# Down projection as seven products, with left factors made beside gate/up and kept in DRAM

## The chip, the cores and the metric

One core of a Trainium2 chip runs the whole program. The metric is the time of one execution in microseconds (us) of device time.

## The reference

The reference is one layer of a streaming encoder, for 1024 prompt rows and 8 x 16 sample rows (1152 rows in all, D = 1024). The change is in its last part, the feed-forward block with 2816 features and the norm behind it:

```python
out = h + (jax.nn.silu(hf @ w_gate) * (hf @ w_up)) @ w_down
y_prompt = rmsnorm(xp, g_final)
y_sample = rmsnorm(xs, g_final)
```

Here `hf` is the normed `h`. Everything is fp32.

## The kernel before

**Products.** Each fp32 operand is split into a high part (ScalarE copies it to the type fp32r, L129) and a low part (VectorE subtracts the high part, L130). `mma` (L881 to L883) then issues three matmuls for each product: high by high, high by low, low by high. The 1152 rows are nine token tiles of 128, or three chunks of 384.

**Gate and up, 1050 to 1518 us.** `swiglu(f0)` handles two of the 22 feature tiles, in 11 steps of 264 matmuls of 384 columns. On chunks 0 and 1 it multiplies by the seven-product form: `head` and `tail` make seven products of quarter matrices in place of eight, with sums and differences of weight quarters (A11, A12, A22, S1 to S4) on one side and of activation quarters (B11, B21, B22, T1 to T4) on the other. Chunk 2 is multiplied plainly (`plain`). `gate` and `up` make the activation `fsg`, and GpSimd's queue stores its six pieces of 128 x 384 per step in the DRAM tensor `a_d` (L1077).

**Down, 1520 to 1799 us.** The products run over two groups of token tiles (5, then 4) and, for each, two halves `dh` of 512 output columns. A pass takes the 22 feature tiles in pairs. For each pair it loads and splits 128 x 1024 of `w_down` (`wd`). In a group's first pass it also loads and splits the activations of that pair from `a_d` (`ar`, into `a`), which stay in SBUF for the second pass. Each token tile has its own PSUM bank (`ps_d`), and takes 22 x 3 matmuls of 512 columns per pass: 9 x 2 x 22 x 3 = 1188 in all. `done(t)` then adds the bank to `y` (L1127), squares and sums on ScalarE (L1131), makes the scale (L1133, L122, a power on GpSimd), scales `y` (L1135) and stores it. In the last pass the last six feature tiles are done token tile by token tile, so that the four tiles finish one after another.

**Order.** A scheduler places each engine's instructions by priority before the run, and each engine then executes its own list in that order. Weight loads and splits get priority over what stands up to `PRI_W` places before them, as far as their buffers allow. A load into a buffer waits until its last reader is done. The pools `wraw`, `whi` and `wlo` (three buffers each) hold weights in all phases; `dp`, `ap2`, `yq` hold `a`, `ar` and `y`. Loads and the stores of `y` are issued on the SyncE queue, in order.

## Time and profile before

| | |
|---|---|
| median of 3 runs | 1797.46 us (1795.79 to 1801.07) |
| profiled execution | 1801.29 us |
| its span, first to last instruction | 1799.5 us |
| mean granted TensorE clock | 0.995 |
| busy share of TensorE, VectorE, ScalarE | 98%, 55%, 33% |

The span is the time that the trace covers; the 1.8 us beside it lie outside any instruction. All times of the trace below are of that one execution. A share of busy time is a mean over the whole program, and single stretches differ from it.

### The profile page before, as it was taken

The page shows a single profiled execution, that of the slowest core. Times are in us where ns is not written, and L with a number is a line of the kernel's source. Part 1 is how long each engine was busy: PE and PEld are TensorE (multiplying, and loading weights), DVE is VectorE, ACT ScalarE, POOL GpSimd, SP SyncE. Part 2 cuts the span into 40 slices and gives each one's busy share as a digit, 9 for nine tenths or more (in the row PEclk, how much of TensorE's full clock was granted, in tenths as well). Part 3 has the DMA queues.
Part 4 walks back from the last instruction along what each step waited for, and adds up shares of the span by engine and source line. Part 5 has one row for each costly group of instructions (what it writes and reads, how often), then busy time and mean ns, then how long its engine had stood idle before and what let it go on. Part 6 is the DMA issues. An engine that isn't in the chain of part 4 may idle for free.

```text
span 1799.5 us, 26106 instructions
## 1 busy us (share of the span) xinstructions
PE 1766.8 (98%) x10503; PEld 1667.8 (93%) x10503; DVE 995.6 (55%) x1739; ACT 600.3 (33%) x1074; POOL 157.0 (9%) x266
## 2 busy tenths in 40 slices
PE   7999999999999999899999899999999999999998
PEld 6998888999999999899999899999999999888886
DVE  6337778464999672543527666555555554433423
ACT  5235556332434322410315423222222222322321
POOL 1020000111121111000001100000000000000000
PEclk9999999999999999999999999999999999999999
DMA  7412112474666435672224311222222224734522
GB/s 220 84 50 70 62 64 67 161 193 140 200 190 194 141 110 144 192 251 86 84 70 152 104 65 62 74 74 74 74 74 74 74 74 158 243 102 158 202 97 70
DMA packets 197285, 214.80 MB, mean 119 GB/s; under 512 B 19699, under 2 KB 162263, under 8 KB 197020
## 3 DMA queue, kind: packets, MB, share of 16 engines
q1 hardware_dynamic: 181228, 161.97, 29.8%
q0 software_dynamic: 15936, 51.17, 8.1%
q8 instruction: 82, 1.34, 0.3%
q14 instruction: 39, 0.32, 0.1%
HBM read 156.63 MB, written 57.39 MB: 119 GB/s over the span
## 4 chain that ended last, share of the span: by engine, by line
PE 92%; DMA 3%; DVE 2%; issue 1%; ACT 1%; POOL 0%; SPq 0%; POOLq 0%; ACTq 0%; DVEq 0%
PE ps_mm L153 11%; PE ps_mm L155 11%; PE ps_mm L154 11%; PE ps_c L882 5%; PE ps_c L883 5%; PE ps_c L881 5%; PE ps_d L881 5%; PE ps_d L882 5%; PE ps_d L883 5%; PE ps_b L883 3%; PE ps_b L882 3%; PE ps_b L881 3%; PE ps_h L883 2%; PE ps_h L881 2%; PE ps_h L882 2%; PE ps_a L881 2%
## 5 line engine op out<-in xcount | busy, mean ns | idle before, releaser
L881 PE MATMUL ps_d<-wd_h,a 128*128 128x512 f32 x396 | 154.7, 391 | 2.1 <-ACT a L129 2.1
L882 PE MATMUL ps_d<-wd_l,a 128*128 128x512 f32 x396 | 154.9, 391 | 0.0
L883 PE MATMUL ps_d<-wd_h,a 128*128 128x512 f32 x396 | 153.5, 390 | 0.0
L130 DVE TENSOR_TENSOR wd_l<-wd_r,wd_h 128x1024 fp32r<-128x1024 f32 x44 | 54.0, 1226 | 152.2 <-ACT wd_h L129 152.2
L129 ACT ACTIVATE wd_h<-wd_r 128x1024 fp32r<-128x1024 f32 x44 | 46.6, 1060 | 181.8 <-PE ps_d L883 160.5
L153 PE MATMUL ps_mm<-T_x,wx_h 128*128 128x384 f32 x288 | 100.0, 347 | 0.0
L155 PE MATMUL ps_mm<-T_x,wx_l 128*128 128x384 f32 x288 | 97.3, 338 | 0.0
L154 PE MATMUL ps_mm<-T_x,wx_h 128*128 128x384 f32 x288 | 97.0, 337 | 0.0
L881 PEld LDWEIGHTS ps_d<-wd_h,a 128*128 128x128 f32 x396 | 74.8, 189 | 18.1 <-ACT a L129 2.5
L882 PEld LDWEIGHTS ps_d<-wd_l,a 128*128 128x128 f32 x396 | 74.8, 189 | 15.7
L883 PEld LDWEIGHTS ps_d<-wd_h,a 128*128 128x128 f32 x396 | 74.6, 188 | 15.4
L1077 POOL DMA_DIRECT2D a_d<-fsg x66 | 35.7, 541 | 478.4 <-DVE fsg L1076 473.1
L1049 DVE TENSOR_TENSOR u<-ps_c,u 128x384 f32<-128x384 f32 x44 | 24.4, 555 | 81.5 <-PE ps_c L883 81.3
L153 PE MATMUL ps_mm<-T_x,wga_h 128*128 128x384 f32 x192 | 65.9, 343 | 0.0
L155 PE MATMUL ps_mm<-T_x,wz_l 128*128 128x384 f32 x192 | 65.2, 340 | 0.0
L153 PE MATMUL ps_mm<-T_x,wz_h 128*128 128x384 f32 x192 | 64.9, 338 | 0.0
L155 PE MATMUL ps_mm<-T_x,wga_l 128*128 128x384 f32 x192 | 64.9, 338 | 0.0
L154 PE MATMUL ps_mm<-T_x,wz_h 128*128 128x384 f32 x192 | 64.8, 338 | 0.0
L153 PE MATMUL ps_mm<-T_x,wgs_h 128*128 128x384 f32 x192 | 64.8, 338 | 0.0
L154 PE MATMUL ps_mm<-T_x,wga_h 128*128 128x384 f32 x192 | 64.7, 337 | 0.0
L154 PE MATMUL ps_mm<-T_x,wgs_h 128*128 128x384 f32 x192 | 64.7, 337 | 0.0
L155 PE MATMUL ps_mm<-T_x,wgs_l 128*128 128x384 f32 x192 | 64.5, 336 | 0.0
(1050 smaller groups left out, 5246.2 us busy)
## 6 DMA issues: line engine op xcount, KB each, us to landing
wd_r<-in_w_down_dram SPq DMA_DIRECT2D x44, 512.0 KB, 3.7
a_d<-fsg POOLq DMA_DIRECT2D x66, 192.0 KB, 2.2
wfg_r<-in_w_gate_dram SPq DMA_DIRECT2D x22, 512.0 KB, 4.1
wfu_r<-in_w_up_dram SPq DMA_DIRECT2D x22, 512.0 KB
acB<-ac_d SPq DMA_DIRECT2D x9, 1024.0 KB, 7.8
ar<-a_d SPq DMA_DIRECT2D x11, 640.0 KB, 5.3
xbc_d<-cv POOLq DMA_DIRECT2D x36, 192.0 KB, 2.1
xb<-xbc_d SPq DMA_DIRECT2D x9, 768.0 KB, 6.4
```

The lines of the kernel that those rows point to most:

```text
L129: act.activation(hi, src, AF.Copy)
L130: vec.tensor_tensor(out=lo, in0=src, in1=hi.bitcast(F32), op=ALU.subtract)
L153: pe.matmul(out, ah, bh, start=(i == 0), stop=False)
L154: pe.matmul(out, ah, bl, start=False, stop=False)
L155: pe.matmul(out, al, bh, start=False, stop=(i == n - 1))
L881: pe.matmul(ps, ah, bh, start=start and i == 0, stop=False, skip_group_check=True)
L882: pe.matmul(ps, ah, bl, start=False, stop=False, skip_group_check=True)
L883: pe.matmul(ps, al, bh, start=False, stop=stop and i == n - 1, skip_group_check=True)
L1049: add = lambda out, ps, x: vec.tensor_tensor(out=out, in0=ps, in1=x, op=ALU.add)
L1077: st(out=a_d[(f0 + i) * P:(f0 + i + 1) * P, c * CW:(c + 1) * CW], in_=t)
```

## The change

The down projection becomes seven products over blocks of a 2 x 2 form: feature halves (11 tiles each), pairs of token tiles (`tA` = 0, 1, 2, 6 and `tB` = 3, 4, 5, 7), and column halves `D1`, `D2`. The order is A11, A12, S1, S4, S2, S3, A22. Each product has 11 steps, and a step has four tile pairs of three matmuls of 512 columns. Tile 8 is multiplied plainly, as a fifth part of the steps of A11, A12, S1 and S4. A11 and A12 share four banks, S1 and S4 another four; S2, S3 and A22 go on adding into a third set of four (printed as `ps_S2`), which is read out after each of the three.

The left factors (sums and differences of activation blocks) are made by `factors` in the gate/up steps, which now pair feature tile f0 with f0 + 11, and are stored in the DRAM tensor `fa_d`, tile 8 in `a8_d`: 16 stores per step in place of 6. Each weight load of gate/up becomes two loads of 256 KB. The buffers of the earlier phases' weights and PSUM are freed ahead of the down phase. In the down phase a step loads 128 x 512 of the left factor and of `w_down` into one `raw` buffer (five of them), and splits both (four `hi` and `lo` buffers). The right factors T1 to T4 are made from `w_down` in place (`t1` to `t4`, by `sub`), with T1 and T2 held in `kept`. Before their last block, products run step by step; the last two steps run tile by tile.

```diff
+HF = NF // 2
+FACTORS = ("A11", "A12", "A22", "S1", "S2", "S3", "S4")
...
-    a_d = dram.tile([FF, T], F32, name="a_d")
+    fa_d = dram.tile([7, HF * P, 512], F32, name="fa_d")
+    a8_d = dram.tile([FF, P], F32, name="a8_d")
...
-            fp = ph2.enter_context(tc.tile_pool(name="fp", bufs=13, reuse_waits="tile"))
+            fp = ph2.enter_context(tc.tile_pool(name="fp", bufs=11, reuse_waits="tile"))
...
-                        ld(out=view(r), in_=src[kh * 512:(kh + 1) * 512, f0 * P:(f0 + 2) * P]
-                           .rearrange("(k p) c -> p k c", p=P))
+                        for j in range(2):
+                            f = (j * HF + f0) * P
+                            ld(out=view(r)[:, :, j * P:(j + 1) * P],
+                               in_=src[kh * 512:(kh + 1) * 512, f:f + P].rearrange("(k p) c -> p k c", p=P))
...
-                    st(out=a_d[(f0 + i) * P:(f0 + i + 1) * P, c * CW:(c + 1) * CW], in_=t)
+                    if i == 1 and c == 2:
+                        factors(*(sg[j, 2][:, n * P:(n + 1) * P] for n in range(2) for j in range(2)), 3 * P, "fs")
+                        for j in range(2):
+                            f = (j * HF + f0) * P
+                            st(out=a8_d[f:f + P, :], in_=sg[j, 2][:, 2 * P:])
+                    elif i == 1 and c == 0:
+                        factors(*(sg[j, n] for n in range(2) for j in range(2)), 0, "ft")
+                def factors(a11, a12, a21, a22, c0, tag):
+                    w = a11.shape[1]
+                    s2_, s3, s4 = (fp.tile([P, w], F32, tag=tag, name=n, bufs=11 if tag == "ft" else 4)
+                                   for n in ("fs2", "fs3", "fs4"))
+                    vec.tensor_tensor(out=s3, in0=a11, in1=a21, op=ALU.subtract)
+                    s1_ = a21
+                    vec.tensor_tensor(out=s1_, in0=a21, in1=a22, op=ALU.add)
+                    vec.tensor_tensor(out=s2_, in0=s1_, in1=a11, op=ALU.subtract)
+                    vec.tensor_tensor(out=s4, in0=a12, in1=s2_, op=ALU.subtract)
+                    for n, x in enumerate((a11, a12, a22, s1_, s2_, s3, s4)):
+                        st(out=fa_d[n, f0 * P:(f0 + 1) * P, c0:c0 + w], in_=x)
...
-            for f0 in range(0, NF, 2):
+            for f0 in range(HF):
...
-        psum_pools(ph, t=5)
...
-        for t0, n in ((0, 5), (5, 4)):
...
+        psum_pools(ph, t=8)
+        def pool(name, bufs=1, **kw):
+            return ph.enter_context(tc.tile_pool(name=name, bufs=bufs, reuse_waits="tile", **kw))
+        fraw, yq, fhl = pool("fraw", 5, side="right"), pool("yq", NT, side="right"), pool("fhl", 4, side="right")
+        xp, keep, yp = pool("xp", 3), pool("keep"), pool("yp", 2)
+        kept = keep.tile([P, HF, 512], F32, name="kept")
+        p1 = [keep.tile([P, 512], F32, name=f"dp1_{p}") for p in range(4)]
+        tA, tB = (0, 1, 2, 6), (3, 4, 5, 7)
+        D1, D2 = slice(0, 512), slice(512, 1024)
+        sub = lambda out, a, b: vec.tensor_tensor(out=out, in0=a, in1=b, op=ALU.subtract)
+        gfB = yp.tile([P, D], F32, name="gfB", bufs=1)
+        ys, sss = [], {}
+        def wd(i, j, f):
+            return w_down[0, (i * HF + f) * P:(i * HF + f + 1) * P, j * 512:(j + 1) * 512]
+        def xload(src, name):
+            x = xp.tile([P, 512], F32, tag=name[:2], name=name)
+            ld(out=x, in_=src)
+            return x
+        def product(left, right, ps, start, stop, a8=None, e=None, estart=False, estop=False, begin=None):
+            steps = []
+            r0 = 512 if a8 is None else 512 + P
...
+            def mm(f, n):
+                h, l, (xh, xl) = steps[f]
+                if n < 4:
+                    c = slice(n * P, (n + 1) * P)
+                    mma(bank_of(n), [(h[:, c], l[:, c], h[:, r0:r0 + 512], l[:, r0:r0 + 512])],
+                        start and f == 0, stop and f == HF - 1)
+                elif a8 is not None:
+                    c = slice(512, r0)
+                    mma(e, [(h[:, c], l[:, c], xh, xl)], estart and f == 0, estop and f == HF - 1)
+            for f in range(HF):
+                with tc.high_priority(max(0, min(PRI_W, tc.cur_priority - pri0[0]))):
+                    raw = fraw.tile([P, 1152], F32, tag="raw", name=f"{left}_{f}_r")
+                    hi = fhl.tile([P, 1152], F32R, tag="hi", name=f"{left}_{f}_h")
+                    lo = fhl.tile([P, 1152], F32R, tag="lo", name=f"{left}_{f}_l")
+                    ld(out=raw[:, :512], in_=fa_d[FACTORS.index(left), f * P:(f + 1) * P, :])
+                    if a8 is not None:
+                        ld(out=raw[:, 512:r0], in_=a8_d[(a8 * HF + f) * P:(a8 * HF + f + 1) * P, :])
+                    rs = slice(r0, r0 + 512)
+                    at, other = right(f, raw[:, rs]) or (None, None)
+                    if at is None:
+                        split(hi[:, :r0 + 512], lo[:, :r0 + 512], raw[:, :r0 + 512])
                     else:
...
+                        split(hi[:, :r0], lo[:, :r0], raw[:, :r0])
+                        split(hi[:, rs], lo[:, rs], at)
+                    x = hi[:, rs], lo[:, rs]
+                    if other is not None:
+                        x = tuple(xp.tile([P, 512], F32R, tag=f"x{n}", name=f"x{n}_{f}") for n in "hl")
+                        split(*x, other)
+                steps.append((hi, lo, x))
+                if f < HF - 2:
+                    for n in range(5):
+                        mm(f, n)
+                if begin is not None and f == 5:
+                    begin()
+            for n in range(5):
+                mm(HF - 2, n)
+                mm(HF - 1, n)
+                yield n
+        def add(t, cols, x):
+            vec.tensor_tensor(out=ys[t][:, cols], in0=x, in1=ys[t][:, cols], op=ALU.add)
+        def square(t, cols):
+            if t not in sss:
+                sss[t] = sm.tile([P, 2], F32, tag="ssf", name="ssf", bufs=NT)
+            n = cols.start // 512
+            sq = yp.tile([P, 512], F32, tag="sq", name="sqf")
+            act.activation(sq, ys[t][:, cols], AF.Square, accum_out=sss[t][:, n:n + 1])
+        def finish(t):
+            ss, y = sss[t], ys[t]
+            vec.tensor_tensor(out=ss[:, 0:1], in0=ss[:, 0:1], in1=ss[:, 1:2], op=ALU.add)
+            r = rstd_of(ss[:, 0:1], 1)
+            vec.scalar_tensor_tensor(out=y, in0=y, scalar=r, in1=gfB, op0=ALU.mult, op1=ALU.mult)
+            ld(out=y_prompt[0, t * P:(t + 1) * P, :] if t < NT - 1 else ys_flat, in_=y)
...
+        def plain(i, j):
+            def right(f, r):
+                ld(out=r, in_=wd(i, j, f))
+            return right
+        def t1(f, r):
+            b11, b12 = xload(wd(0, 0, f), "ba"), xload(wd(0, 1, f), "bb")
+            sub(kept[:, f, :], b12, b11)
+            return kept[:, f, :], b12
+        def t2(f, r):
+            ld(out=r, in_=wd(1, 1, f))
+            sub(kept[:, f, :], r, kept[:, f, :])
+            return kept[:, f, :], None
+        def t3(f, r):
+            ld(out=r, in_=wd(1, 1, f))
+            sub(r, r, xload(wd(0, 1, f), "bb"))
+        def t4(f, r):
+            ld(out=r, in_=wd(1, 0, f))
+            sub(r, r, kept[:, f, :])
+        def total(p, ps):
+            u = yp.tile([P, 512], F32, tag="u", name="du")
+            vec.tensor_tensor(out=u, in0=ps, in1=p1[p], op=ALU.add)
+            return u
+        a, c, b = ([None] * 4 for _ in range(3))
+        e = bank("t", "ps_e1")
+        for n in product("A11", plain(0, 0), a, True, False, a8=0, e=e, estart=True, begin=load_y):
+            if n < 4:
+                act.activation(p1[n], a[n], AF.Copy)
+        for n in product("A12", plain(1, 0), a, False, True, a8=1, e=e, estop=True):
+            if n < 4:
+                add(tA[n], D1, a[n])
+                square(tA[n], D1)
+            else:
+                add(8, D1, e)
+                square(8, D1)
+        e = bank("t", "ps_e2")
+        for n in product("S1", t1, c, True, False, a8=0, e=e, estart=True):
+            if n < 4:
+                add(tB[n], D2, c[n])
+        for n in product("S4", plain(1, 1), c, False, True, a8=1, e=e, estop=True):
+            if n < 4:
+                add(tA[n], D2, c[n])
+            else:
+                add(8, D2, e)
+                square(8, D2)
+                finish(8)
+        for n in product("S2", t2, b, True, False):
+            if n < 4:
+                add(tA[n], D2, total(n, b[n]))
+                square(tA[n], D2)
+                finish(tA[n])
+                add(tB[n], D1, p1[n])
+        for n in product("S3", t3, b, False, False):
+            if n < 4:
+                add(tB[n], D2, total(n, b[n]))
+                square(tB[n], D2)
+        for n in product("A22", t4, b, False, True):
+            if n < 4:
+                add(tB[n], D1, b[n])
+                square(tB[n], D1)
+                finish(tB[n])
```

Three places of VectorE's list follow. The first is where the third product into a set of banks follows the second (S3 to A22). `A22_k_r`, `_h` and `_l` are the raw, high and low buffers of step k; `du` is the sum that `total` makes from a bank; numbers at the end count the tiles. Before, at the end of a pass, the list had this:

```order
L130 TENSOR_TENSOR wd5_1_0_l_15399<-wd5_1_0_r_15396,wd5_1_0_h_15398 128x1024
L130 TENSOR_TENSOR wd5_1_2_l_15429<-wd5_1_2_r_15426,wd5_1_2_h_15428 128x1024
L1127 TENSOR_TENSOR y5_15130<-ps_d_14990,y5_15130 128x512
L1127 TENSOR_TENSOR y6_15132<-ps_d_14991,y6_15132 128x512
L1127 TENSOR_TENSOR y7_15134<-ps_d_14992,y7_15134 128x512
L1127 TENSOR_TENSOR y8_15136<-ps_d_14993,y8_15136 128x512
L130 TENSOR_TENSOR wd5_1_4_l_15459<-wd5_1_4_r_15456,wd5_1_4_h_15458 128x1024
L130 TENSOR_TENSOR wd5_1_6_l_15489<-wd5_1_6_r_15486,wd5_1_6_h_15488 128x1024
L130 TENSOR_TENSOR wd5_1_8_l_15519<-wd5_1_8_r_15516,wd5_1_8_h_15518 128x1024
```

Now it has this, where products A22 and S3 meet:

```order
L1135 TENSOR_TENSOR A22_5_r_16222<-A22_5_r_16222,kept_14359 128x512
L1246 TENSOR_TENSOR du_16080<-ps_S2_15568,dp1_0_14360 128x512
L1246 TENSOR_TENSOR du_16092<-ps_S2_15572,dp1_1_14361 128x512
L134 TENSOR_TENSOR A22_2_l_16164<-A22_2_r_16162,A22_2_h_16163 128x1024
L1198 TENSOR_TENSOR y3_14514<-du_16080,y3_14514 128x512
L1135 TENSOR_TENSOR A22_6_r_16242<-A22_6_r_16242,kept_14359 128x512
L1198 TENSOR_TENSOR y4_14516<-du_16092,y4_14516 128x512
L134 TENSOR_TENSOR A22_3_l_16184<-A22_3_r_16182,A22_3_h_16183 128x1024
L1246 TENSOR_TENSOR du_16104<-ps_S2_15576,dp1_2_14362 128x512
L1246 TENSOR_TENSOR du_16116<-ps_S2_15580,dp1_3_14363 128x512
```

The reads of the four banks (L1246) are no longer a group by themselves: two splits, a `sub` and two additions stand between the second and the third of them.

The second place is where S3 follows S2, again on VectorE; `bb` is the second block of `w_down` that T3 needs. The counterpart before is the list shown first.

```order
L134 TENSOR_TENSOR S3_1_l_15880<-S3_1_r_15878,S3_1_h_15879 128x1024
L1246 TENSOR_TENSOR du_15786<-ps_S2_15568,dp1_0_14360 128x512
L1135 TENSOR_TENSOR S3_5_r_15966<-S3_5_r_15966,bb_15971 128x512
L1246 TENSOR_TENSOR du_15805<-ps_S2_15572,dp1_1_14361 128x512
L1198 TENSOR_TENSOR y0_14508<-du_15786,y0_14508 128x512
L1198 TENSOR_TENSOR y1_14510<-du_15805,y1_14510 128x512
L1246 TENSOR_TENSOR du_15824<-ps_S2_15576,dp1_2_14362 128x512
L1135 TENSOR_TENSOR S3_6_r_15988<-S3_6_r_15988,bb_15993 128x512
L1246 TENSOR_TENSOR du_15843<-ps_S2_15580,dp1_3_14363 128x512
L134 TENSOR_TENSOR S3_2_l_15902<-S3_2_r_15900,S3_2_h_15901 128x1024
```

Here the `sub` of S3_6, which needs the raw buffer that S3_1's split gives back, stands ahead of the read of the fourth bank.

The third place is the end of VectorE's list. Before:

```order
L1133 TENSOR_TENSOR ssf_15381<-ssf_15381 128x1
L1135 SCALAR_TENSOR_TENSOR y5_15130<-y5_15130,rs_r_15678,gfB_14216 128x1024
L122 TENSOR_SCALAR rs_v_15704<-ssf_15381 128x1
L1127 TENSOR_TENSOR y7_15134<-ps_d_15394,y7_15134 128x512
L1135 SCALAR_TENSOR_TENSOR y6_15132<-y6_15132,rs_r_15706,gfB_14216 128x1024
L1133 TENSOR_TENSOR ssf_15385<-ssf_15385 128x1
L122 TENSOR_SCALAR rs_v_15732<-ssf_15385 128x1
L1135 SCALAR_TENSOR_TENSOR y7_15134<-y7_15134,rs_r_15734,gfB_14216 128x1024
L1127 TENSOR_TENSOR y8_15136<-ps_d_15395,y8_15136 128x512
L1133 TENSOR_TENSOR ssf_15389<-ssf_15389 128x1
L122 TENSOR_SCALAR rs_v_15760<-ssf_15389 128x1
L1135 SCALAR_TENSOR_TENSOR y8_15136<-y8_15136,rs_r_15762,gfB_14216 128x1024
```

Now, with L1198 adding, L1209 and L126 making the scale's input and L1211 scaling:

```order
L1198 TENSOR_TENSOR y5_14518<-ps_S2_15576,y5_14518 128x512
L1209 TENSOR_TENSOR ssf_16095<-ssf_16095 128x1
L1211 SCALAR_TENSOR_TENSOR y3_14514<-y3_14514,rs_r_16330,gfB_14364 128x1024
L126 TENSOR_SCALAR rs_v_16344<-ssf_16095 128x1
L1198 TENSOR_TENSOR y7_14522<-ps_S2_15580,y7_14522 128x512
L1209 TENSOR_TENSOR ssf_16107<-ssf_16107 128x1
L1211 SCALAR_TENSOR_TENSOR y4_14516<-y4_14516,rs_r_16346,gfB_14364 128x1024
L126 TENSOR_SCALAR rs_v_16360<-ssf_16107 128x1
L1209 TENSOR_TENSOR ssf_16119<-ssf_16119 128x1
L126 TENSOR_SCALAR rs_v_16376<-ssf_16119 128x1
L1211 SCALAR_TENSOR_TENSOR y5_14518<-y5_14518,rs_r_16362,gfB_14364 128x1024
L1211 SCALAR_TENSOR_TENSOR y7_14522<-y7_14522,rs_r_16378,gfB_14364 128x1024
```

The scalings of three tiles (y4, y5, y7) now stand behind the last addition from a bank; before, only that of the last tile (y8) did.

## Rows read from the trace of the kernel before

**Rows 1.** The page: span, and busy time by engine.
```profile
span 1799.5 us, 26106 instructions
PE 1766.8 (98%) x10503; PEld 1667.8 (93%) x10503; DVE 995.6 (55%) x1739; ACT 600.3 (33%) x1074; POOL 157.0 (9%) x266
```

**Rows 2.** The page: chain that ended last, by engine.
```profile
PE 92%; DMA 3%; DVE 2%; issue 1%; ACT 1%; POOL 0%; SPq 0%; POOLq 0%; ACTq 0%; DVEq 0%
```

**Rows 3.** Windows: busy us and instructions by engine, granted clock, DMA share, GB/s.
```profile
core 0: us, PE busy (x) PEld busy (x) DVE busy (x) ACT busy (x) POOL busy (x), PEclk, DMA share, GB/s
1050.00:1300.00 250.00, 250.00 (x1432) 250.00 (x1431) 145.53 (x219) 68.10 (x90) 17.82 (x33) 1.00 0.23 75
...
1518.40:1520.60 2.20, 0.07 (x2) 0.04 (x1) 1.86 (x4) 2.20 (x3) 0.54 (x1) 1.00 0.15 49
1520.60:1526.00 5.40, 5.40 (x17) 4.29 (x18) 2.84 (x3) 1.08 (x1) 0.00 (x0) 0.68 0.96 313
...
1592.60:1661.00 68.40, 68.40 (x303) 56.66 (x302) 25.00 (x25) 22.46 (x29) 0.00 (x0) 1.00 0.41 139
...
1728.00:1791.40 63.40, 63.40 (x282) 52.45 (x280) 20.48 (x26) 14.29 (x23) 1.65 (x3) 1.00 0.22 73
```

**Rows 4.** Waits of 1520 to 1800 us: total, times, longest.
```profile
ACT wd_h L129 <- PE ps_d L883: 160.5, 37, 5.7
...
ACT a L129 <- DMA ar<-a_d: 11.4, 6, 5.7
```

**Rows 5.** PE's order of time around the start of the down phase.
```profile
1518.10 0.34 PE L883 MATMUL ps_c<-T_h,wfu_l 128*128 128x384 f32 x1
1520.57 0.50 PE L881 MATMUL ps_d<-wd_h,a 128*128 128x512 f32 x1 [2.13 <-ACT a L129]
```

**Rows 6.** Groups of 1520 to 1800 us, shapes apart: busy, mean ns, idle before.
```profile
L130 DVE TENSOR_TENSOR wd_l<-wd_r,wd_h 128x1024 fp32r<-128x1024 f32 x42 | 51.5, 1226 | 149.3 <-ACT wd_h L129 149.3
L129 ACT ACTIVATE wd_h<-wd_r 128x1024 fp32r<-128x1024 f32 x41 | 43.5, 1060 | 161.2 <-PE ps_d L883 160.5 <-DMA y<-h_d 0.7
L130 DVE TENSOR_TENSOR a<-ar,a 128x1280 fp32r<-128x1280 f32 x11 | 16.2, 1491 | 10.7 <-ACT a L129 10.5
...
L1127 DVE TENSOR_TENSOR y<-ps_d,y 128x512 f32<-128x512 f32 x18 | 12.2, 687 | 9.4 <-PE ps_d L883 9.3
L1135 DVE SCALAR_TENSOR_TENSOR y<-y,rs_r,gfB 128x1024 f32<-128x1024 f32 x9 | 11.5, 1281 | 1.5 <-POOL rs_r L124 1.5
...
L1133 DVE TENSOR_TENSOR ssf<-ssf 128x1 f32<-128x1 f32 x9 | 1.4, 152 | 1.4 <-ACT sqf L1131 1.4
```

**Rows 7.** Groups of earlier stretches: smaller tensor operations, the stores, a weight's split.
```profile
L763 DVE TENSOR_TENSOR t<-t,yb 128x512 f32<-128x512 f32 x16 | 10.3, 681 | 0.0
...
L130 DVE TENSOR_TENSOR ohl<-oc,ohl 128x128 fp32r<-128x128 f32 x12 | 2.7, 288 | 10.2 <-ACT ohl L129 10.2
...
L1077 POOL DMA_DIRECT2D a_d<-fsg x66 | 35.7, 541 | 478.4 <-DVE fsg L1076 473.1
...
L129 ACT ACTIVATE wfu_h<-wfu_r 128x1024 fp32r<-128x1024 f32 x20 | 21.2, 1061 | 20.0 <-PE ps_c L882 20.0
```

**Rows 8.** DMA issues: count, KB each, median us from issue to landing.
```profile
wd_r<-in_w_down_dram SPq DMA_DIRECT2D x44, 512.0 KB, 3.7
...
y<-h_d SPq DMA_DIRECT2D x9, 512.0 KB, 6.6
...
oc<-o_d SPq DMA_DIRECT2D x3, 256.0 KB, 4.3
...
h<-in_x_sample_dram SPq DMA_DIRECT2D x1, 512.0 KB, 10.2
```

**Rows 9.** A window of 2 us in which the DMA engines were full.
```profile
1530.00:1532.00 2.00, 2.00 (x10) 1.67 (x9) 1.37 (x2) 0.85 (x2) 0.00 (x0) 1.00 1.05 421
```

**Rows 10.** PE's last matmul and VectorE's last rows, in order of time.
```profile
1788.32 1.28 DVE L1135 SCALAR_TENSOR_TENSOR y<-y,rs_r,gfB 128x1024 f32<-128x1024 f32 x1
1789.51 0.15 DVE L1133 TENSOR_TENSOR ssf<-ssf 128x1 f32<-128x1 f32 x1
...
1791.37 0.39 PE L883 MATMUL ps_d<-wd_h,a 128*128 128x512 f32 x1
...
1794.40 1.28 DVE L1135 SCALAR_TENSOR_TENSOR y<-y,rs_r,gfB 128x1024 f32<-128x1024 f32 x1 [0.73 <-POOL rs_r L124]
```

83 lines of the change are left out of this document (16 added, 67 removed).

## The prediction

> **What bounds the kernel now.** I read the page first: TensorE is busy 1766.8 of 1799.5 us [rows 1], and the chain of work that ended last lies on it for 92% [rows 2]. The windows say the same for both stretches that the change touches: in gate/up 250.00 of 250.00 us, and in the middle of the down phase 68.40 of 68.40 us, at a granted clock of 1.00, the upper of the two levels [rows 3]. VectorE and ScalarE have room there: 25.00 and 22.46 us of 68.40. The waits show the direction: ScalarE waits 160.5 us for matmuls to give weight buffers back, and only 11.4 us for the loads of activations [rows 4]. So in the down phase TensorE sets the pace and the others follow. From 1592.6 to 1661 us a matmul takes 68.40 / 303 = 0.226 us.
>
> The profiled execution took 1801.29 us, 1.8 more than its span, and the median of the runs is 3.8 lower. I sum against the span of 1799.5 and take off 2.0 for the median.
>
> **What it removes.** 1188 matmuls become 7 x 4 x 11 x 3 = 924, and 4 x 11 x 3 = 132 for tile 8: 1056. The 132 fewer are worth 132 x 0.226 = **29.8 us**, as long as nobody keeps TensorE waiting. A step of four tiles is now 12 x 0.226 = 2.71 us, one with tile 8 is 3.39. The rest asks whether the others keep that pace.
>
> **Gate/up: 0.** Per step (264 matmuls; 250 us hold 1432, so 46 us) VectorE gets four operations on 384 columns, at no more than the 0.68 of 512 columns, and four on 128 columns at about 0.29 [rows 7]: at most 3.9 us on 145.53 / 250 x 46 = 26.8 us [rows 3]. GpSimd gets 16 stores of 0.54 us [rows 7], 8.7 us of 46. No instruction of gate/up reads a factor back, and the down phase begins with the oldest ones. Weight loads become 256 KB in 512-byte rows; a 256-KB load landed in 4.3 us [rows 8], and today the split of those weights waits for TensorE and never for its load [rows 7]. So this work lies beside the matmuls. If that cover failed at some steps, 3 us in all; the term is 0 to +3, and I take 0.
>
> **The start: -1.** Today TensorE idles 2.1 us for ScalarE's first `a` [rows 5], and its clock then falls: 0.68 in the next 5.4 us [rows 3], worth 5.4 x 0.32 = 1.7. Now the raw and high parts of the first steps can be ready before gate/up ends, since their buffers lie over activations that are done earlier. VectorE has, after the last gate/up matmul, one product of 384 columns (at most 0.68), three of 128 columns (0.29 each) and the low part of A11_0, 1152 columns wide: between 1.23 and 1.49, so 1.36 [rows 6]. That is 2.9 us, and five high-by-high matmuls (1.1 us) run in it. The idle becomes about 1.6 us, in two pieces. With the clock lost as today it is -0.5, without -2.2, with one late load +3. I take -1.
>
> **Inside the seven products: +7.** Now each product loads and splits both factors anew. VectorE per step: A11, A12, S4 one split of 1152 columns, 1.36 us of 3.39; S1 three splits and a `sub`, 2.9 of 3.39; S2 two splits and a `sub`, 2.0 of 2.71; S3 and A22 one split of 1024 (1.23) and a `sub` (0.68), 1.9 of 2.71 [rows 6, 7]. To S3 and A22 come four scalings (1.28), 16 reads and additions (0.69) and eight small operations (0.15): 22 x 1.91 + 5.1 + 11.0 + 1.2 = 59.3 us in 22 x 2.71 = 59.6. VectorE's rows follow each other some 0.08 us closer than their lengths (1788.32 + 1.28 against 1789.51, rows 10), which gives about 6 us back. So VectorE has next to no room there, and where it comes late in its list's order TensorE waits.
>
> Where S3 ends, the list shows a wait that no speed of the loads removes. A22_2 needs the buffers of S3_9 (four of them, in turn), which are free when S3's last block ends. Then follow ScalarE's high part (1.06) and A22_2_l (1.23), an addition, a `sub`, an addition, A22_3_l, and only then the third `du`. From the end of S3: 1.06 - 0.6 for the earlier end of S3_9, then 1.15 + 0.61 + 0.60 + 0.61 + 1.15 + 0.69 = 5.3 us. TensorE wants that bank (A22_0, third tile) 6 x 0.226 = 1.36 us after S3's end. It waits **3.9 us**.
>
> Where S2 ends, the `sub` of S3_6 stands ahead of the fourth `du`. Its load can start when S3_1_l is done, at about 1.3 us before S2's end; with 4.3 us of landing [rows 8] the `sub` ends 3.7 us after that end and the `du` 0.6 later, where TensorE wants it at 2.0: 2.3 us late. With 2 us of landing there is no wait; with 6.6, the time of a `y` load in traffic [rows 8], it is 4.6. Further on S3_5 stands behind three scalings and two `sub`s, 0 to 3 us late; I take 1. The sum is 3.9 + 2.3 + 1, about 7, with 3 (the list alone, fast loads) and 16 (6.6 us at the five links of this kind) as ends.
>
> The DMA engines carry it. The down phase moves 77 + 99 loads of 256 KB, 44 of 64 KB, `y`, `gfB` and the output, about 59 MB, in 248 us: 238 GB/s, where full engines gave 421 [rows 9]. S3 is densest: 33 loads, 8.7 MB, and 2 MB of output in 30 us, 360 GB/s.
>
> **The tail: +1.6.** Today the last matmul starts at 1791.37 and the last scaling ends at 1795.68 [rows 10], 3.9 us after that matmul's end; the store takes the remaining 3.8. Now three scalings stand behind the last addition: by the list, 0.85 us after the end VectorE is free of y3, and then an addition 0.61, 1.2, small ones 0.5, 1.2 and 1.28, 5.5 us in all. Bounds are 1 and 4, the latter with four stores at once.
>
> **Sum:** 1799.5 - 29.8 + 0 - 1 + 7 + 1.6 = 1777.3; less 2.0 gives **1775** us. With all favourable ends it is 1797.5 - 29.8 - 2.2 + 3 + 1 = 1769.5, and the pace of a matmul (0.225 to 0.227) moves that by 0.1 only; with the unfavourable ones 1797.5 - 29.8 + 3 + 3 + 16 + 4 = 1793.7.
>
> **Rivals.**
> *The chain of late steps is longer (0.2).* In S3, and in S1 where VectorE has 0.5 us per step to spare, each wait for a raw buffer passes on. The 360 GB/s of S3 speak for it, the unused 421 against. With the links at 6.6 us the stalls are 16: 1797.5 - 29.8 - 1 + 16 + 1.6 = 1784; with S1 in it up to 1792.
> *The clock falls at each new wait (0.15).* One idle of 2.1 us was followed by a clock of 0.68 [rows 3, 5] and 1.7 us lost. Waits of 3.9 and 2.3 us could each bring that: 3.4 us, 1779. Against it: these waits come in pieces, between which matmuls run. The Trainium skill, "TensorE: Matmul & The Clock Gate", Part 1, says that the throttled state is the default and activity releases it; by that both waits would cost twice, which is this rival, and the trace agrees in its one case.
> *Slower (0.07): the loads land late.* From S2's middle to S3_4 six links follow one another, in each of which a split gives a raw buffer back, a load lands, a `sub` runs and the next split waits. Beyond 4.3 us every microsecond of landing costs about six. The gain of 22 is gone at 4.3 + 22 / 6 = 8.0 us. A 512-KB load did take 10.2 us once [rows 8]: then 1775 + 6 x 5.9 = 1810. For it speaks that loads are halved in size and doubled in number, against it the 3.7 us of 512-KB weights [rows 8]. The Trainium skill, "DMA: Bandwidth & Descriptors", section "Bandwidth", asks for transfers of 1 MiB or more and so speaks against the whole scheme. The trace does not bear that out so far: loads of 512 and 640 KB filled the engines at 421 GB/s [rows 9].
> *Nothing comes of it (0.03):* if VectorE kept TensorE waiting 1.2 us in each of 22 steps, 26 us, the time would be 1794 to 1799.
>
> **Numbers.** Forecast 0.55, rivals as above. The forecast's own range is 1769 to 1781; up to 1792 with the first two rivals. Two runs of this kernel differ by up to 0.3% (1795.79 to 1801.07), so below 1792.1 counts as faster: all of the forecast and the clock, nearly all of the first rival, 0.88; same 0.05, slower 0.07.
>
> **What would show it.** Right: 1056 matmuls of 512 columns at 0.226 us; no wait of TensorE in gate/up; in its waits two groups, for `du` (L1246) at S2's and S3's ends, of 2 to 5 us; the last scaling ends 5 to 6 us after the last matmul. Wrong: waits for low parts (L134) in every step of S1, S3 or A22, with VectorE in turn waiting for loads; landing times of 256-KB loads over 6 us; idle TensorE in gate/up for weights or for `fsg` buffers; a granted clock below 1 in the down phase.

## The result, and the profile after

The changed kernel takes 1774.15 us (median of four runs, 1772.09 to 1779.35), the kernel before 1798.80 (four runs): a ratio of 0.9868, interval 0.9840 to 0.9897. It is faster by 1.3%. The forecast was 1775, its own range 1769 to 1781, up to 1792 with the first two rivals.

The profiled execution has a span of 1774.2 us, 25.3 less than before [rows 1]. The page of the changed kernel, busy time by engine and the chain that ended last:

```profile
span 1774.2 us, 26800 instructions
PE 1738.3 (98%) x10371; PEld 1641.8 (93%) x10371; DVE 1091.8 (62%) x1935; ACT 625.1 (35%) x1122; POOL 218.0 (12%) x376
...
PE 89%; DMA 5%; DVE 3%; issue 2%; ACT 1%; POOL 1%; SPq 0%; DVEq 0%; POOLq 0%; ACTq 0%
```

Next to the kernel before [rows 1], TensorE has 132 matmuls and 28.5 us of busy time less; VectorE has 96.2 us more and is still far from full over the whole span. Only the windows show where it is nearly full (columns as in rows 3):

```profile
core 0: us, PE busy (x) PEld busy (x) DVE busy (x) ACT busy (x) POOL busy (x), PEclk, DMA share, GB/s
1050.00:1300.00 250.00, 250.00 (x1434) 250.00 (x1433) 162.34 (x263) 68.06 (x91) 46.10 (x86) 1.00 0.29 93
...
1521.00:1526.00 5.00, 5.00 (x24) 4.12 (x23) 4.43 (x4) 1.17 (x1) 0.58 (x2) 1.00 0.80 245
1526.00:1560.00 34.00, 34.00 (x152) 28.16 (x151) 20.05 (x22) 14.71 (x17) 0.00 (x0) 1.00 1.04 385
...
1690.00:1720.00 30.00, 28.76 (x124) 22.84 (x124) 25.54 (x38) 12.85 (x19) 5.18 (x4) 1.00 0.75 249
1720.00:1750.00 30.00, 28.20 (x124) 22.89 (x123) 25.45 (x32) 13.22 (x19) 0.47 (x1) 1.00 0.63 209
```

Gate/up is as full as before, with 1434 matmuls in its 250 us instead of 1432, although VectorE's share there went from 145.53 to 162.34 us and GpSimd's from 17.82 to 46.10. In the down phase the 34 us from 1526 on run without a gap beside full DMA engines. The last two windows lie in the end of S2, in S3 and in A22: VectorE is busy 25.5 of 30 us, and TensorE is idle for 1.2 and 1.8 us of them. These are all waits of TensorE in the down phase that the view of waits lists (total, times, longest):

```profile
PE ps_S L885 <- DVE du L1246: 1.8, 1, 1.8
PE ps_S L886 <- DVE S_l L134: 1.1, 1, 1.1
PE ps_A L886 <- DVE A_l L134: 0.8, 1, 0.8
PE ps_A L885 <- DVE fsg L1082: 0.7, 1, 0.7
```

The same four in TensorE's order of time, with what stood ahead of two of them (an idle time there can be some 0.2 us longer than the wait in brackets):

```profile
1517.09 0.34 PE L887 MATMUL ps_c<-T_h,wfu_l 128*128 128x384 f32 x1
1518.17 1.17 PE L885 MATMUL ps_A<-A_h 128*128 128x512 f32 x4 [0.74 <-DVE fsg L1082]
...
1520.32 0.50 PE L886 MATMUL ps_A<-A_l,A_h 128*128 128x512 f32 x1 [0.76 <-DVE A_l L134]
...
1716.05 0.50 PE L886 MATMUL ps_S<-S_l,S_h 128*128 128x512 f32 x1 [1.15 <-DVE S_l L134]
...
1731.37 0.39 PE L887 MATMUL ps_S<-S_h,S_l 128*128 128x512 f32 x1
1733.56 0.47 PE L885 MATMUL ps_S<-A_h 128*128 128x512 f32 x1 [1.80 <-DVE du L1246]
...
1763.45 0.39 PE L887 MATMUL ps_S<-A_h,A_l 128*128 128x512 f32 x1
```

The last wait is at the place where S3 hands its banks to A22. VectorE's own order of time around it:

```profile
1730.78 0.69 DVE L1135 TENSOR_TENSOR A_r<-A_r,kept 128x512 f32<-128x512 f32 x1 [0.66 <-DMA A_r<-in_w_down_dram]
1732.12 0.69 DVE L1135 TENSOR_TENSOR A_r<-A_r,kept 128x512 f32<-128x512 f32 x1 [0.65 <-DMA A_r<-in_w_down_dram]
1732.73 1.28 DVE L1246 TENSOR_TENSOR du<-ps_S,dp 128x512 f32<-128x512 f32 x2
1733.93 1.21 DVE L134 TENSOR_TENSOR A_l<-A_r,A_h 128x1024 fp32r<-128x1024 f32 x1
...
1736.87 1.22 DVE L134 TENSOR_TENSOR A_l<-A_r,A_h 128x1024 fp32r<-128x1024 f32 x1
1738.00 1.28 DVE L1246 TENSOR_TENSOR du<-ps_S,dp 128x512 f32<-128x512 f32 x2
```

S3's last matmul starts at 1731.37. The first read of a bank (`du`) starts only at 1732.73, behind two `sub`s that each waited for a load. The third read starts at 1738.00, 6.4 us after S3's end, the fourth follows it, and TensorE does not wait for them.

The DMA issues show the loads in their new sizes (count, KB each, median us to landing):

```profile
S_r<-fa_d SPq DMA_DIRECT2D x44, 256.0 KB, 2.8
...
A_r<-fa_d SPq DMA_DIRECT2D x33, 256.0 KB, 5.0
...
A_r<-in_w_down_dram SPq DMA_DIRECT2D x33, 256.0 KB, 4.4
...
S_r<-in_w_down_dram SPq DMA_DIRECT2D x33, 256.0 KB, 3.6
...
bb<-in_w_down_dram SPq DMA_DIRECT2D x22, 256.0 KB, 3.7
```

And the last rows of VectorE, behind TensorE's last matmul:

```profile
1764.45 0.68 DVE L1198 TENSOR_TENSOR y<-ps_S,y 128x512 f32<-128x512 f32 x1
...
1767.34 2.48 DVE L1211 SCALAR_TENSOR_TENSOR y<-y,rs_r,gfB 128x1024 f32<-128x1024 f32 x2 [0.48 <-POOL rs_r L128]
```

The 25.3 us, by the two profiled executions:

| Part | Forecast | Measured | From |
|---|---|---|---|
| Up to the last gate/up matmul | 0 | -1.0 | 1518.10 [rows 5] to 1517.09 |
| 132 matmuls fewer | -29.8 | -29.9 | 132 x 0.2267, the pace of before |
| Start of the down phase | -1 | -2.0 | idle and lost clock, 4.0 before, 2.0 after |
| Inside the products | +7 | +5.0 | four pieces of waiting, 4.0, and 0.2276 us a matmul in place of 0.2267 between them |
| Tail | +1.6 | +2.6 | last matmul's end to the span's end, 7.74 to 10.36 |
| Sum | -22.2 | -25.3 | |

The four pieces inside the products are 0.26 us where S2 meets S3, 1.32 within S3, 1.96 where S3 meets A22, and 0.5 in small ones.

### The profile page after: what moved, and what is told of

The parts are those of the page before. It is cut to its first block, busy times and chain, and to the rows that moved or that the text cites. A ratio compares the mean times of both kernels' runs of the same rounds, so it can differ in the third digit from the quotient of the medians.

```text
span 1774.2 us, 26800 instructions
## 1 busy us (share of the span) xinstructions
PE 1738.3 (98%) x10371; PEld 1641.8 (93%) x10371; DVE 1091.8 (62%) x1935; ACT 625.1 (35%) x1122; POOL 218.0 (12%) x376
## 4 chain that ended last, share of the span: by engine, by line
PE 89%; DMA 5%; DVE 3%; issue 2%; ACT 1%; POOL 1%; SPq 0%; DVEq 0%; POOLq 0%; ACTq 0%
PE ps_mm L157 11%; PE ps_mm L159 11%; PE ps_mm L158 11%; PE ps_c L886 5%; PE ps_c L887 5%; PE ps_c L885 5%; PE ps_b L887 3%; PE ps_b L886 3%; PE ps_b L885 3%; PE ps_h L886 2%; PE ps_h L885 2%; PE ps_h L887 2%; PE ps_S L885 2%; PE ps_S L887 2%; PE ps_S L886 2%
## 5 line engine op out<-in xcount | busy, mean ns | idle before, releaser
L1102 POOL DMA_DIRECT2D fa_d<-fsg x88 | 47.4, 541 | 360.1 <-DVE fsg L1082 354.5
L1055 DVE TENSOR_TENSOR u<-ps_c,u 128x384 f32<-128x384 f32 x44 | 24.5, 556 | 79.3 <-PE ps_c L887 78.9
L886 PE MATMUL ps_S<-S_l,S_h 128*128 128x512 f32 x176 | 68.7, 391 | 1.1 <-DVE S_l L134 1.1
L887 PE MATMUL ps_S<-S_h,S_l 128*128 128x512 f32 x176 | 68.4, 390 | 0.0
L128 POOL TENSOR_TENSOR rs_r<-rs_v,mhalf 128x1 f32<-128x1 f32 x36 | 30.5, 851 | 289.0 <-DVE rs_v L126 287.4
L133 ACT ACTIVATE S_h<-S_r 128x640 fp32r<-128x640 f32 (+3 forms) x44 | 39.3, 898 | 74.7 <-PE ps_e L887 26.6
L885 PE MATMUL ps_S<-S_h 128*128 128x512 f32 x176 | 64.5, 391 | 0.1
L159 PE MATMUL ps_mm<-T_y,ws_l 128*128 128x384 f32 x192 | 64.6, 336 | 0.0
L157 PE MATMUL ps_mm<-T_y,ws_h 128*128 128x384 f32 x192 | 64.6, 336 | 0.0
L158 PE MATMUL ps_mm<-T_y,ws_h 128*128 128x384 f32 x192 | 64.5, 336 | 0.0
```

The source lines that it names most:

```text
L128: gps.tensor_tensor(out=r, in0=v, in1=mhalf[:, :n], op=ALU.pow)
L133: act.activation(hi, src, AF.Copy)
L157: pe.matmul(out, ah, bh, start=(i == 0), stop=False)
L158: pe.matmul(out, ah, bl, start=False, stop=False)
L159: pe.matmul(out, al, bh, start=False, stop=(i == n - 1))
L885: pe.matmul(ps, ah, bh, start=start and i == 0, stop=False, skip_group_check=True)
```

## The experiments

**The theory** was that what is left inside the products comes from the order of VectorE's list at banks that one product hands to the next. **The first rival** was that the chain of raw buffers and loads (split, load, `sub`, split) does it; **the second** that TensorE's clock does. The gate/up phase of one and the same kernel turned out to last a few us more or less from one execution to the next (last section), so single traces are compared below from the start of the last gate/up matmul to the span's end. That stretch is 281.40 us before and 257.11 in the changed kernel; in two more executions of the changed kernel (below) it is 258.5 and 258.3. So a difference of a microsecond between two single traces says nothing; the waits themselves, with their places, say more.

**1. The gate/up part alone.** The factors and the row order are made as in the changed kernel; `a_d` is still stored, and the down phase is that of before.

```diff
+                    g = i * HF + f0
-                    st(out=a_d[(f0 + i) * P:(f0 + i + 1) * P, c * CW:(c + 1) * CW], in_=t)
+                    st(out=a_d[g * P:(g + 1) * P, c * CW:(c + 1) * CW], in_=t)
...
-            for f0 in range(0, NF, 2):
+            for f0 in range(HF):
```

> The gate/up part of the change by itself (features paired f0 with f0 + 11, 256-KB weight loads, factors made and stored in fa_d and a8_d), with the down phase of before reading a_d; so GpSimd issues 22 stores a step. Theory (the added work lies beside the matmuls): no wait of TensorE in gate/up, time as before within 0.3%, last gate/up matmul within 1.5 us of before's 1518.10. Rival (VectorE, the stores or the smaller loads hold gate/up up, and the down phase's gain was larger than it looks): 3 us or more later at that matmul, time 3 to 6 us above before.

Measured: 1800.68 us (ten runs) against 1796.54 (thirteen), ratio 1.0023 (1.0013 to 1.0033). TensorE waits nowhere in gate/up for the added work. The last gate/up matmul starts at 1514.71, 3.4 us earlier than in the trace of before and outside the 1.5 expected, but not later; the first of the down phase starts 2.47 after it, as before. So gate/up does not pay for the factors in this trace. What is longer is the very end: from the last matmul's end to the span's end 11.54 us pass instead of 7.74, and the last 5 of these hold neither an instruction nor a transfer:

```profile
1793.30:1798.30 5.00, 0.00 (x0) 0.00 (x0) 0.00 (x0) 0.00 (x0) 0.00 (x0) 0.50 0.00 0
```

The medians differ by 4.1 us, as the rival had it (3 to 6), though not in gate/up: this end is 3.8 longer in the trace. Why is not shown. The changed kernel's end is 2.6 longer than before (table), and most of that lies in its scalings.

**2. T3 and T4 without their `sub`.** The loads stay, the subtractions on VectorE go.

```diff
-            sub(r, r, xload(wd(0, 1, f), "bb"))
+            xload(wd(0, 1, f), "bb")
...
-            sub(r, r, kept[:, f, :])
```

> The changed kernel without the subtractions that make T3 and T4 (the loads stay; S3 and A22 multiply by the plain blocks). VectorE has 22 x 0.68 = 15 us less to do in the last 60 us. Theory (VectorE's work and its list make TensorE wait in S3 and A22): the waits of 1.3 us inside S3 and 2.0 us where S3 meets A22 go, together with the 0.4 at S3's begin, span 3 to 4 us below the changed kernel's 1774.2. Rival (the loads land late, VectorE only passes it on): the splits wait for the loads instead, and 2 us or more of waits stay.

Measured: one run, 1777.21 us, in an execution whose gate/up was long (last matmul at 1522.57). From there to the end 252.83 us, 4.3 less than the changed kernel. The waits in S3 and at S3's end are gone; of 1.13 us of idle time after the first matmul of the down phase 0.93 is the second piece of the start. So these waits hang on the `sub`s. The run does not separate VectorE's time for them from its own waits for their loads (0.65 and 0.66 us above), since both go together.

**3. A22 in banks of its own.** S3's sums are read once and added to both halves of `y`; A22 starts in four other banks.

```diff
-        for n in product("S3", t3, b, False, False):
+        for n in product("S3", t3, b, False, True):
...
-                add(tB[n], D2, total(n, b[n]))
+                u = total(n, b[n])
+                add(tB[n], D2, u)
...
+                add(tB[n], D1, u)
-        for n in product("A22", t4, b, False, True):
+        for n in product("A22", t4, d, True, True):
```

> The changed kernel with A22 in four banks of its own, so that its first matmuls need no read of S3's banks; VectorE adds S3's sum to both column halves, with the same number of operations. Theory (the 2.0 us between S3 and A22 are the wait for the first read of a bank, which stands behind a subtraction that waits for its load): that wait goes, span about 2 us lower, and the rest is unchanged. Rival (VectorE is full there, so it comes late anyway): the 2 us come back within A22 as waits for low parts.

Measured: one run, 1770.06 us; 255.02 from gate/up to the end, 2.1 less. The 1.96 us where S3 meets A22 are gone, and they do not come back within A22. The wait within S3 stays, 1.31 with its start:

```profile
1712.26 0.50 PE L886 MATMUL ps_S<-S_l,S_h 128*128 128x512 f32 x1 [1.14 <-DVE S_l L134]
```

The number of `sub`s, splits and loads is the same, so the hand-over of banks is what the 1.96 us hung on. Together with run 2: both the `sub` ahead of `du` and the shared bank are needed for the wait.

**4. The last four steps of A22 tile by tile**, to bring the first three scalings forward.

```diff
-                if f < HF - 2:
+                if f < HF - late:
...
-        for n in product("A22", t4, b, False, True):
+        for n in product("A22", t4, b, False, True, late=4):
```

> The changed kernel with the last four steps of A22 done token tile by token tile in place of two, so that the last four tiles finish 2.72 us apart in place of 1.36. Theory (the tail is 2.6 us longer than before because 2.3 us of VectorE work per tile do not fit in 1.36 us): the end comes 7.5 to 8.5 us after the last matmul in place of 10.4, and VectorE's last scaling ends 4 us after it in place of 6.0. Rival (the four stores, together on the DMA engines, set the tail): 10 us as now.

Measured: one run, 1781.70 us (gate/up long again, last matmul at 1521.96); 257.94 from there. The last scaling ends 5.88 us after the last matmul, where the changed kernel has 5.98: no gain. VectorE's row shows why:

```profile
1766.18 1.89 DVE L1198 TENSOR_TENSOR y<-ps_S,y 128x512 f32<-128x512 f32 x3 [4.89 <-PE ps_S L887]
```

VectorE adds three tiles in a row, because TensorE's last matmuls for them still come together: they start at 1765.76, 1766.21 and 1766.66. That the scheduler does so because the split of step 10 comes late is argued, not shown.

**5. Four raw buffers instead of five**, which makes each load start later.

```diff
-        fraw, yq, fhl = pool("fraw", 5, side="right"), ...
+        fraw, yq, fhl = pool("fraw", 4, side="right"), ...
```

> The changed kernel with four raw buffers in place of five, so that each load of the down phase can be issued one step later. Theory (the chain of buffer, load, subtraction and split has little to spare where S2, S3 and A22 meet, as in the rival that prices six links): the waits of TensorE from S2's end on grow from 3.5 us to 8 us or more. Rival (loads are ahead everywhere and VectorE's list alone decides): 3 to 5 us, as now. Compared from the last gate/up matmul on, since the pace of gate/up differs from run to run.

Measured: one run, 1780.19 us, 260.36 from gate/up to the end, 1.9 to 3.2 more than the changed kernel's three traces. The waits from S2's end on are 1.35, 1.67 and 0.67, 3.7 in all, much as with five buffers (the rival's 3 to 5, not the 8 or more of the theory). The new ones are elsewhere, in A11 and A12, where the loads of `y` run:

```profile
1552.01 1.20 PE L885 MATMUL ps_A<-A_h 128*128 128x512 f32 x4 [0.96 <-ACT A_h L133]
...
1560.73 1.19 PE L885 MATMUL ps_A<-A_h 128*128 128x512 f32 x4 [1.39 <-ACT A_h L133]
```

So the number of raw buffers does not set the waits in S3 and A22, although VectorE still stands idle for loads there (0.84 us for the `sub` ahead of the first `du`); fewer buffers bind first in the part where the DMA engines are full.

**6. Own banks, and half of the last scalings off VectorE.** As run 3; besides, the second halves of the last tiles are multiplied by `gfB` early, and ScalarE scales them at the end.

```diff
+            for t in tB:
+                vec.tensor_tensor(out=ys[t][:, D2], in0=ys[t][:, D2], in1=gfB[:, D2], op=ALU.mult)
...
+                vec.scalar_tensor_tensor(out=y[:, D1], in0=y[:, D1], scalar=r, in1=gfB[:, D1], op0=ALU.mult, op1=ALU.mult)
+                act.activation(y[:, D2], y[:, D2], AF.Copy, scale=r)
```

> The changed kernel with A22 in its own banks and a shorter tail: the second column half of the last four tiles is multiplied by the final gain during A22 on VectorE, and ScalarE scales that half at the end beside VectorE. Theory: the wait of 2.0 us between S3 and A22 goes, the last scaling ends 4 to 5 us after the last matmul in place of 6.0, the 1.3 us in S3 stay: 3 to 4 us less than the changed kernel. Rival (VectorE's four more operations in A22 make low parts late there): the gain is 1 us or none.

Measured: 1772.73 us (four runs, 1771.22 to 1774.38), ratio 0.9868 (0.9855 to 0.9880). 254.85 from gate/up to the end. The last scaling ends 4.92 us after the last matmul instead of 5.98, but the four stores now come together: the DMA engines are full for 4 us (share 1.00 to 1.05), and the whole tail stays at 10.5 us. In the trace the gain over the changed kernel is that of run 3, not the 3 to 4 us expected. The interval of the times lies within that of the result, 0.9840 to 0.9897.

**7. As run 6, with the `gfB` products and the scalings of the first tiles on GpSimd and ScalarE.**

```diff
+                gps.tensor_tensor(out=y, in0=y, in1=gfB, op=ALU.mult)
+                act.activation(y, y, AF.Copy, scale=r)
```

> As the run with own banks and the shorter tail, and the scalings of the four tiles that end with S2 taken off VectorE: GpSimd multiplies by the gain, ScalarE scales; GpSimd also makes the multiplications of the last tiles' second half. No row here shows a GpSimd operation on 128 x 1024. Theory (VectorE's three scalings ahead of S3_5's split cause the 1.3 us): that wait goes too, 4 to 6 us less than the changed kernel. Rival (GpSimd is so slow that ScalarE, which waits for its result ahead of the split of S3_7, holds S3 up): waits of 2 us or more in S3.

Measured: 1780.20 us (six runs, 1769.83 to 1784.18), ratio 0.9900 (0.9879 to 0.9920); 260.7 from gate/up to the end, where 4 to 6 us less than the changed kernel were expected. The waits of TensorE sum to 8.8 us, the start included; one of them, in A22, is 3.28 us long, and the granted clock is 0.66 over the 5 us behind it, some 1.7 us more. GpSimd's row, and VectorE's beside it:

```profile
1706.49 5.21 POOL L1212 TENSOR_TENSOR y<-y,gfB 128x1024 f32<-128x1024 f32 x2 [27.44 <-ACT sqf L1205]
```

```profile
1707.01 2.44 DVE L1135 TENSOR_TENSOR S_r<-S_r,bb 128x512 f32<-128x512 f32 x1
...
1709.38 0.68 DVE L1253 TENSOR_TENSOR du<-ps_S,dp 128x512 f32<-128x512 f32 x1
...
1709.98 2.81 DVE L134 TENSOR_TENSOR S_l<-S_r,S_h 128x1024 fp32r<-128x1024 f32 x1
```

A `sub` takes 2.44 us in place of 0.69, a split 2.81 in place of 1.22; `du`, one of whose inputs is a bank, keeps its 0.68. So two GpSimd operations cost VectorE 1.75 and 1.59 us here, each more than the scaling of 1.28 that it was to save. The Trainium skill, "SBUF — State Buffer", section "SBUF: two separate sides", says that a VectorE operation with two inputs in SBUF and a GpSimd operation that reads SBUF exclude each other at a shared port, for the whole length of the one that comes first; these rows agree.

**8, 9 and 10. The two kernels again**, unchanged.

> The changed kernel once more, beside the others of this call. Theory (the pace of gate/up matmuls differs between executions of the same program): the last gate/up matmul starts at another time than 1517.1, by up to 5 us, while from there to the end it takes 256 to 258 us as in the first trace. Rival (it was the code of the variants that changed the pace): 1517 within 0.5 us.

> The changed kernel a third time, beside the other two of this call. Theory: 256 to 258.5 us from the last gate/up matmul to the end; the clock stays at its upper level after the wait between S3 and A22 or falls, as it did in one of two traces. Rival (the runs differ as much in the down phase): outside 255 to 260.

> The kernel before once more, for a second trace. Theory (whether the granted clock falls after a wait of 2 us differs between executions, as between two traces of the changed kernel, and the first profiled execution of before was a long one): the down phase from the last gate/up matmul on takes 279.5 to 281.5 us, with or without the 1.7 us at the low clock, and the span is 2 to 5 us below 1799.5, mostly from phases ahead of gate/up. Rival (the first trace is typical): span within 1 us of 1799.5, with the low clock at the start of the down phase.

Measured: the changed kernel 1778.77 us (five runs), ratio 0.9884 (0.9866 to 0.9902), and 1774.77 (six), ratio 0.9872 (0.9851 to 0.9893); the kernel before 1801.59, one run with its profile. In the two traces of the changed kernel the wait where S3 meets A22 is 2.10 and 2.23 us, the one within S3 1.32 and 1.34, and the one at S2's end 0.17 and 0.85. In the first of the two the clock fell behind S3's end:

```profile
1734.00:1736.70 2.70, 0.82 (x4) 0.36 (x2) 1.72 (x4) 1.06 (x1) 0.00 (x0) 1.00 0.63 213
1736.70:1740.20 3.50, 3.44 (x9) 2.69 (x10) 3.50 (x6) 0.74 (x3) 0.00 (x0) 0.53 0.22 61
1740.20:1744.00 3.80, 3.80 (x18) 3.16 (x17) 3.80 (x6) 0.93 (x3) 0.00 (x0) 0.98 0.65 219
```

Nine matmuls in 3.5 us instead of fifteen: some 1.4 us lost. In the second, after the longer wait, it did not fall. In the kernel before it fell once (0.68, rows 3) and did not fall in the repeat, after the same 2.3 us of idle time; nor in run 1, which has the same down phase. The repeat takes 279.86 us from gate/up to the end, 1.5 less than the first trace. Its span, 1799.8, is not the 2 to 5 us shorter that was expected, since its gate/up ended later (1519.96). All runs of each kernel together: 1797.32 before (39), 1775.62 after (15).

**11. The p1 sums added early.** `p1` is added to `y` in A12, so that the banks of S2 and S3 are added directly, without `du`; A22 has banks of its own.

```diff
                 act.activation(p1[n], a[n], AF.Copy)
+                for t, cols in ((tA[n], D2), (tB[n], D2), (tB[n], D1)):
+                    add(t, cols, p1[n])
...
-                add(tA[n], D2, total(n, b[n]))
+                add(tA[n], D2, b[n])
```

> The changed kernel with the first product's sums added to y during A12, where VectorE has room, so that the banks of S2 and S3 are added to y directly; A22 has banks of its own. VectorE has four reads less to do at S2's end. Theory (VectorE's list where S2, S3 and A22 meet makes the waits): the 1.3 us inside S3, the 2.0 us between S3 and A22 and the small wait at S2's end go, 3 to 4 us less from the last gate/up matmul to the end than the 257 to 258.5 us of the changed kernel, so 253.5 to 254.5. Rival (the same work at another place makes A12 or S1 wait): the sum of waits stays above 3 us.

Measured: 1775.97 us (six runs, 1766.05 to 1779.24), ratio 0.9865 (0.9841 to 0.9888); 255.44 from gate/up to the end. The 1.3 us within S3 and the 1.96 at its end are gone, but 0.82 stands at S2's end and a new wait of 1.39 in A22. I had expected 253.5 to 254.5: the waits taken away came back in part at other places of VectorE's list. The `sub`s and their loads are the same, and run 3, with own banks alone, keeps the 1.3 us within S3. So those hung on the reads and additions ahead of that split, or on the order of the list that comes with them.

**12. Tile 8 left out of most steps**, to see S1 at the pace of four tiles.

```diff
-                elif a8 is not None:
+                elif a8 is not None and f in (0, HF - 1):
```

> The changed kernel without the matmuls of token tile 8 in all steps but the first and last of A11, A12, S1 and S4: 108 matmuls left out, its loads and splits stay. Theory (time is matmuls times 0.227 us as long as VectorE keeps up, and in S1 it needs 2.9 us of a step that is now 2.71): 24.5 us less less what S1 loses, 2 to 4 us, so 232 to 237 us from the last gate/up matmul to the end, with waits for low parts in S1. Rival (VectorE keeps up there too, since its instructions overlap): 232 us and no wait in S1.

Measured: one run, 1753.14 us; 236.98 from gate/up to the end, 21.3 less than the 258.3 of one trace of the changed kernel, where 108 matmuls are worth 24.5. The sum lies in the expected range, but not for the expected reason: no wait appeared in S1. The run doesn't test S1 either. With the matmuls of tile 8 gone, hardly anything reads the splits that are made for it alone, and all eleven of them are done by 1582.9, while A12 still runs; from 1590 to 1606.2 VectorE is busy for 9.8 of 16.2 us, 1.6 us per step and not 2.9. The waits came in A12, beside the loads of `y` and this earlier work, and in S3 and A22 (1.70, 1.31, 1.91).

## Why the prediction was right, and which step of it failed

**The matmuls** make the result: 132 fewer, at 0.2267 us each, -29.9 against -29.8. **Gate/up** costs nothing, as forecast: no wait of TensorE there, 1434 matmuls in 250 us against 1432, and run 1 repeats it by itself. The -1.0 us up to its end arises for the most part ahead of 1040 us and is less than what the end of gate/up scatters by from one execution to the next (last section).

**The start** went as described, in two pieces (0.91 us for the last `fsg`, 0.92 for the first low part) with five high-by-high matmuls between them. The term was -2.0 instead of -1, because the clock stayed at 1.00; I had taken a value between the bound with the clock lost and the bound without. Of the 2.0, 1.7 is the low clock of that one execution of before, which two other traces of the same down phase don't have (run 1 and the repeat).

**Inside the products** the sum was near (5.0 for 7), but **the step that failed is the one behind its two largest terms: when TensorE wants a bank.** The largest is the 3.9 us of "a wait that no speed of the loads removes" at the third bank of A22_0. It assumed that TensorE does A22's first step on all four banks before the second, and so wants the third bank 1.36 us after S3's end. VectorE's list was read as it stands, TensorE's was not. Its list of the changed kernel says otherwise (rows between left out; 15568, 15572 and 15576 are the first three banks, `A_3` is step 3 of A22):

```
L885 MATMUL ps_S_15568<-A_0_h 128x512
...
L885 MATMUL ps_S_15572<-A_0_h 128x512
...
L885 MATMUL ps_S_15568<-A_3_h 128x512
L885 MATMUL ps_S_15572<-A_3_h 128x512
L886 MATMUL ps_S_15568<-A_3_l,A_3_h 128x512
L887 MATMUL ps_S_15568<-A_3_h,A_3_l 128x512
L886 MATMUL ps_S_15572<-A_3_l,A_3_h 128x512
L887 MATMUL ps_S_15572<-A_3_h,A_3_l 128x512
L885 MATMUL ps_S_15576<-A_0_h 128x512
```

Steps 0 to 3 run on two banks, 24 matmuls or 5.4 us, before the third bank is touched. The trace agrees: the matmul that waits for VectorE's third read starts at 1739.18, 24 matmuls after the first of A22. The third read came even later than I had worked out (6.4 us after S3's end, not 4.6), and nobody waited for it. The wait that did come, 1.96 us, is for the first read, behind two `sub`s that waited for their loads; I had priced none there. Run 3 removes it by other banks, run 2 by taking the `sub`s away.

**S2's end** cost 0.26 us instead of 2.3, and the same step failed there. These rows of SyncE, VectorE and TensorE stand around it; S2's last matmul starts at 1699.35:

```profile
1695.42 0.42 SPq L1237 DMA_DIRECT2D S_r<-in_w_down_dram  x1
```

```profile
1697.20 0.68 DVE L1246 TENSOR_TENSOR du<-ps_S,dp 128x512 f32<-128x512 f32 x1
1699.85 0.69 DVE L1135 TENSOR_TENSOR S_r<-S_r,bb 128x512 f32<-128x512 f32 x1 [1.97 <-issue]
1700.46 0.68 DVE L1246 TENSOR_TENSOR du<-ps_S,dp 128x512 f32<-128x512 f32 x1
...
1703.46 0.68 DVE L1246 TENSOR_TENSOR du<-ps_S,dp 128x512 f32<-128x512 f32 x1
```

```profile
1701.20 0.50 PE L885 MATMUL ps_S<-S_h 128*128 128x512 f32 x1
```

The fourth read ends 4.6 us after S2's end, where I had worked out 4.3, and it isn't waited for: by the semaphores that TensorE waits for, it touches the fourth bank only at 1704.75, 21 matmuls and 5.2 us after S2's end, and not after 2.0. The 0.26 is for the second read, behind the `sub` of S3_5. That `sub` stood still until its load had landed (the view names no releaser, the semaphores it waits for do), 4.4 us after its issue at 1695.42; so the landing time that I had taken, 4.3, was right.

**S3_5** cost 1.32, forecast 1, at the place named. The rest, some 1.5 us, is small change: short gaps and a pace that is 0.0009 us slower per matmul.

So of the 7 us inside the products 6.2 stood for two waits that did not come. In their place came 1.96, 0.26 and the small change, for reads and gaps that had not been priced. That the sum is only 2 us off is luck; the 29.8 us of matmuls are not.

**The tail** was 1 us more than forecast: the last scaling ends 5.98 us after the last matmul (5.5 forecast), and 4.4 us follow it instead of 3.8. Run 6 shows that the scalings alone aren't what the end waits for: 1 us less of them gave nothing, since the stores then meet on full DMA engines.

**The rivals.** The longer chain of late steps did not come: from 1690 to 1735 us the median landing times of 256-KB loads are 3.0 to 4.5 us, the 4.9 to 5.9 from 1522 to 1575 made TensorE wait for nothing, and run 5, which makes loads later, put no more wait into S3. The slow case needed 8 us of landing; the Trainium skill's rule of 1 MiB or more ("DMA: Bandwidth & Descriptors", section "Bandwidth"), which spoke for it, is not borne out here: transfers of mostly 256 KB moved 385 GB/s at a DMA share of 1.04. The clock rival is true in some executions: it cost nothing in the profile of the result and 1.4 us in a repeat. Of the signs named for being right, the waits for `du` at S2's and S3's ends, 2 to 5 us each, did not come as described (0.26 and 1.96).

What stays open: how much of the wait where S3 meets A22 is VectorE's own time and how much its waits for loads (run 2 takes both away; in the trace 1.31 us of idle time for loads stand right ahead of the first `du`), and what the end without instructions waits for (run 1). Within S3 the trace and run 11 speak for VectorE's own work: it is busy without a gap from 1708.71 until the split that TensorE waits for, though a wait of 0.76 for a load stands ahead of that. None of the variants is clearly faster than the changed kernel, though runs 3, 6 and 11 save 2 us or so behind gate/up in their traces.

## What to carry to other kernels

Where a product is traded for operations on another engine, count the matmuls first; here their term came out to 0.1 us, and everything else together was 4.6. Then look for the few places where that engine's list puts new work ahead of the read that frees a bank, and read both lists there, the one that frees and the one that wants, since a scheduler may have reordered the second so that a late read costs nothing. Part of what is so removed can come back at the next full spot, of the same engine (run 11) or of the stores (run 6), and here GpSimd was no place for VectorE's overflow, both reading SBUF (run 7).
